# The order of a retention head's five projection blocks: v moved behind both gate blocks, and to second place in the last head

## The chip, the cores and the metric

The kernel runs on one core of a Trainium2 chip. The time is the device time of one execution in microseconds (us); smaller is better. Engines are named as the profile names them: PE (matmuls), PEld (the weight loads of PE), DVE, ACT, POOL, and SP, which here only issues DMAs. PSUM is the memory that matmuls write, SBUF the one that all engines read.

## The reference

A trunk of two layers on 1024 tokens of width 1024, in float32. What the change touches is the mixer of layer 1, a retention with 4 heads, of key width 256 and value width 512:

```python
def retention_mixer(xn, wq, wk, wv, wg, gn_gain, wo):
    ...
    q = (xn @ wq).reshape(Bn, S, RET_HEADS, RET_KDIM)
    k = (xn @ wk).reshape(Bn, S, RET_HEADS, RET_KDIM) * (RET_KDIM ** -0.5)
    v = (xn @ wv).reshape(Bn, S, RET_HEADS, RET_VDIM)
    o = chunkwise_retention(rotary(q, pos), rotary(k, pos), v)
    ...
    return (jax.nn.silu(xn @ wg) * o) @ wo
```

A head so has a `q` and a `k` of 256 columns, a `v` of 512 and a gate `g` of 512. The five projections of a head, and those of different heads, can be computed in any order.

## The kernel before, in words

**Blocks.** The projections of a head are five blocks of PE's work. `q`, `k`, and the gate in two halves (`g0` and `g2`, 256 columns each) are one call of `strassen` each: seven products of Strassen's scheme with 12 matmuls of 128x512 each, 84 in all. `values_block` computes `v`: seven products of 48 matmuls of 128x256. Every operand is split in a high and a low part: a cast on ACT (L109) and a subtraction on POOL or DVE (L110) make an `hl` tile out of a `raw` one (a weight as it was loaded) or an `s` tile (a sum or difference of weights, on DVE). PE starts on a product when its `hl` is there and its PSUM bank is free. The products of one block go into four banks (`b` or `o`, in turn by block), some banks twice; L284, L300, L305 and L311 are ACT's copies out of them into `u`, L289, L310, L312 and L315 are DVE's additions to `u`. L300 and L305 free banks that the same block uses again.

**Buffers.** `raw` has 5 slots (L126 loads one, SP issues), `hl` 7, `s` 3, `u` 5, and `h` one. `h` is used by the rotation and, as `extra`, by `values_block` for half of its sums.

**The rotation.** After `q` and after `k`, `rotated(h, s, us)` applies the rotary tables in two halves: DVE multiplies into `h` (L1151), adds into `u` (L1152, L1153), ACT casts and DVE subtracts (L109, L110, into `h`), and ACT issues the write of `h` to the scratch tensor `qscr` (L1158, 1 MB; for `k` two more writes of `u` to `kscr`, L1157, 256 KB each). Half 1 needs the same `h` tile, so it waits until half 0's `qscr` write has landed. PE is meanwhile in the next block. A gate block ends in two silu activations (L1324) and two writes to `scr` (L1325), and `v`'s results go to `vscr` (L1087, 512 KB each).

**Order.** All engines and queues take their instructions in order, and a scheduler has merged the blocks' steps: loads, casts and sums of the next block stand among the steps of the one that runs. Before, every head has the order `q`, `k`, `g0`, `v`, `g2`, with banks `b`, `o`, `b`, (`v` takes both), `o`. The very last `g2` is given to `last_block`, which frees parts of `xc` (the split activations) as it goes and fetches the first unit's `q`, `k`, `kf`, `v` from the scratch tensors (L1165, L1171, L1174, L1276).

**The units.** After the blocks the retention itself runs in eight units (4 heads, 2 halves of the tokens): `scores` (L1186 matmuls, L1191 on DVE, split into `sT`), `key_rows` (L1201 transposes, L1202 and L1203 into `ky`), `first_state` (L1212 matmuls, L1218 and L1219 into `st`), `outputs` (L1236 matmuls, L1240 statistics, L1227 scaling into `ky`), `gated` (L1260 transposes). Weights `wo` of the output projection are loaded beside them as `raw`.

Of the kernel before, what the change touches and what calls it, by code (L numbers as in the profile page):

```python
# [13 lines left out]
P = 128  # L14
# [60 lines left out]
def trunk(tc, a):  # L75
# [28 lines left out]
    def f(ap):  # L104
        return ap.bitcast(F32)

    def split(hi, lo, src, eng=None):

        act.copy(hi, src)  # L109
        (eng or pool).tensor_tensor(lo, src, f(hi), ALU.subtract)  # L110
# [227 lines left out]
    def run(gen):  # L338
        for _ in gen:
            pass  # L340
# [294 lines left out]
    def filler():  # L635
        for c in range(4):
            while at["heads"] <= c:
                yield
            yield from gated_conv(c)
        while at["values"] < 4 or at["pairs"] < 3:  # L640
            yield
        vp.close()
        xtp.close()
        mix["mp"] = Pool("mp")
        mix["ab"] = Pool("ab")
        gather((1, 3, 5, 7, 0, 2, 4), mix["ab"])
        for js in ((1, 3), (5, 7)):
            for _ in project(js, (1, 3, 5, 7, 0, 2, 4, 6), u_bank):
                yield from (None,) * 4

    steps = filler()
# [57 lines left out]
    def xc_tiles():  # L709
        return [xcp[b].tile([P, 2, 4, HALF], "xc", dt=F32R) for b in range(7)]  # L710
# [3 lines left out]
    def u_tile():  # L714
        return mp.tile([P, T], "u", 5)

    def h_tile():
        return mp.tile([P, 2, T], "h", dt=F32R)
# [65 lines left out]
    xc = xc_tiles()  # L784
# [251 lines left out]
    xc = nxt["xc"]  # L1036
# [105 lines left out]
    def rotated(h, s, us):  # L1142

        for half in range(2):
            tab = u_tile().rearrange("p (a t) -> p a t", a=2)
            sync.dma_start(out=tab, in_=a["c_rot"][h, half, :, 2 * s : 2 * s + 2, :])
            cs, sn = tab[:, 0, :], tab[:, 1, :]
            u0, u1 = (u[:, half * HALF : (half + 1) * HALF] for u in us)
            hl = h_tile().rearrange("p s (a t) -> p s a t", a=2)
            for i, (x, y) in enumerate(((u0, cs), (u1, sn), (u0, sn), (u1, cs))):  # L1150
                dve.tensor_tensor(f(hl[:, i // 2, i % 2]), x, y, ALU.mult)  # L1151
            dve.tensor_tensor(u0, f(hl[:, 0, 0]), f(hl[:, 0, 1]), ALU.subtract)  # L1152
            dve.tensor_tensor(u1, f(hl[:, 1, 0]), f(hl[:, 1, 1]), ALU.add)  # L1153
            for i, u in enumerate((u0, u1)):
                split(hl[:, 0, i], hl[:, 1, i], u, dve)
                if s == 1 and half == 0:
                    act.dma_start(out=kscr[h, :, i], in_=u)  # L1157
            act.dma_start(out=qscr[4 * h + 2 * half + s], in_=f(hl))  # L1158
# [106 lines left out]
    def wo_sweep(half, h, yT, g, tiles, after=None):  # L1265
        def lhs(j):
            return lambda s, t: yT[2 * g + j][:, s, (t - 4 * half) * P : (t - 4 * half + 1) * P]

        return sweep(
            [lhs(j) for j in range(2)], [w_rows(wo, h * 4 + 2 * g + j) for j in range(2)], tiles, o_bank, after  # L1270
        )
# [14 lines left out]
    def last_block(steps):  # L1286

        yield next(steps)
        close_xc(0)
        rt[0] = Pool("rt0")  # L1290
        unit0["q"] = fetch_q(0, 0)
        unit0["tri"] = wk.tile([P, HALF], "g", 2)
        sync.dma_start(out=unit0["tri"], in_=a["c_tri"])
        yield next(steps)
        close_xc(1)
        rt[1] = Pool("rt1")
        unit0["k"] = fetch_k(0, 0)
        yield next(steps)
        close_xc(6)
        rt[2] = Pool("rt2")  # L1300
        unit0["v"] = fetch_v(0, 0, sync)
        yield from steps
        close_xc(4, 3, 5, 2)
        rt[3] = Pool("rt3")
        rt[4] = Pool("rt4")

    blocks = [("ret_wq", 0), ("ret_wk", 0), ("ret_wg", 0), None, ("ret_wg", 2)]
    for h in range(4):
        for n, block in enumerate(blocks):
            if block is None:  # L1310
                run(values_block(h))
                continue
            name, i = block
            c0 = (h * (4 if name == "ret_wg" else 2) + i) * P
            us = []
            steps = strassen(a[name][0], c0, c0 + P, xc, Both, ((o_bank if n in (1, 4) else b_bank),), us, lay=1)
            if h == n == 0:
                steps, us = nxt["head"]
            run(last_block(steps) if (h, n) == (3, 4) else steps)
            if n < 2:  # L1320
                rotated(h, n, us)
                continue
            for j, u in enumerate(us):
                act.activation(u, u, AF.Silu)  # L1324
                act.dma_start(out=scr[4 * h + i + j], in_=u)  # L1325
# [5 lines left out]
    steps = iter(())  # L1331
    for n, (h, half) in enumerate(units):
# [24 lines left out]
        if more:  # L1357
            gt = fetch_g(*units[n + 1])
            tiles = range(4 * half, 4 * half + 4)
            steps = chain(*[wo_sweep(half, h, yT, g, tiles) for g in range(2)])  # L1360
# [3 lines left out]
    xc = xc_tiles()  # L1364
# [53 lines left out]
```

## Time and profile before

| | |
|---|---|
| time, median of 3 runs | 2725.92 us (2721.56 to 2728.98) |
| profiled execution | 2726.38 us, of which the span of the trace is 2724.6 us |
| PE busy | 2645.2 us, 97% of the span |
| DVE, ACT, POOL busy | 1915.8, 1189.9, 795.9 us |
| retention projections | 1243.8 to 1708.8 us of the span |

A row of the timeline has the start and the duration of an instruction, or of several alike in succession (x12), and in brackets the engine's idle time before it and what ended it. "<-ACT u L305" means that ACT's instruction of line 305, which wrote or read a `u` tile, came last.

### The profile page before, as it was taken

How to read it: one execution, taken by the hardware profiler on the slowest of the kernel's cores; microseconds unless marked ns; L12 is line 12 of the kernel's file. 1: busy time of each engine (PE TensorE's matmuls, PEld its weight loads, DVE VectorE, ACT ScalarE, POOL GpSimd, SP SyncE). 2: the span in 40 equal slices, each digit the busy share in tenths (PEclk: the TensorE clock that was granted, in tenths of full speed). 3: DMA queues.
4: the chain of work that ended last, by engine and by line, in shares of the span. 5: the costliest groups of instructions: out<-in, count | busy, mean ns of one | idle time of the engine just before them, and what ended most of it. 6: DMA issues, size and time to landing. Idle time of an engine off the chain costs nothing. (4 is left out here: it accounts for less than half of the span.)

```text
span 2724.6 us, 34990 instructions
## 1 busy us (share of the span) xinstructions
PE 2645.2 (97%) x12793; PEld 2166.0 (80%) x12793; DVE 1915.8 (70%) x2950; ACT 1189.9 (44%) x2050; POOL 795.9 (29%) x603
## 2 busy tenths in 40 slices
PE   8999999899999999989999999899999999999999
PEld 6877777778888888868888888788877888887887
DVE  4247776687777789697575765466678777777986
ACT  4345543454444444364444434222235444445444
POOL 6721113533333400032222122344454333331000
PEclk9999999999999999999999999899999999999999
DMA  5310012122222274424554546655422222225654
GB/s 171 104 48 28 24 35 79 38 75 89 74 89 74 86 266 154 152 84 160 176 178 151 195 150 219 244 210 186 155 73 60 78 85 72 88 74 187 206 174 154
DMA packets 258785, 336.74 MB, mean 124 GB/s; under 512 B 15121, under 2 KB 182197, under 8 KB 252469
## 3 DMA queue, kind: packets, MB, share of 16 engines
q1 hardware_dynamic: 224428, 246.94, 28.4%
q10 hardware_dynamic: 34184, 87.57, 8.8%
q8 instruction: 100, 1.64, 0.2%
q14 instruction: 73, 0.59, 0.1%
HBM read 257.38 MB, written 77.07 MB: 123 GB/s over the span
## 5 line engine op out<-in xcount | busy, mean ns | idle before, releaser
L110 POOL TENSOR_TENSOR hl<-raw,hl 128x512 fp32r<-128x512 f32 x347 | 580.9, 1688 | 1250.9 <-ACT hl L109 1231.0
L245 PE MATMUL b<-xc,hl 128*128 128x512 f32 (+1 forms) x2652 | 606.2, 388 | 10.7 <-ACT u L305 5.7
L245 PE MATMUL o<-xc,hl 128*128 128x512 f32 (+1 forms) x2568 | 590.7, 389 | 12.9 <-DVE hl L110 3.3
L245 PEld LDWEIGHTS b<-xc,hl 128*128 128x128 f32 x2652 | 485.9, 189 | 125.2 <-ACT u L305 7.0
L245 PEld LDWEIGHTS o<-xc,hl 128*128 128x128 f32 x2568 | 473.4, 190 | 123.6 <-DVE hl L110 4.2
L109 ACT CAST hl<-raw 128x512 fp32r<-128x512 f32 (+1 forms) x440 | 264.9, 609 | 508.7 <-PE o L328 151.7
L110 DVE TENSOR_TENSOR hl<-s,hl 128x512 fp32r<-128x512 f32 x309 | 223.6, 727 | 222.0 <-ACT hl L109 222.0
L972 DVE SCALAR_TENSOR_TENSOR u<-u,cc,u 128x1022 f32<-128x1022 f32 (+1 forms) x176 | 263.4, 1521 | 0.9
L109 ACT CAST hl<-s 128x512 fp32r<-128x512 f32 x309 | 189.7, 619 | 136.8 <-PE b L245 47.2
L458 PE MATMUL u<-xT,hl 128*128 128x512 f32 x576 | 166.1, 410 | 0.0
L328 PE MATMUL o<-hl,y 128*128 128x512 f32 x672 | 163.6, 397 | 0.0
L905 PE MATMUL o<-hl,hl 128*128 128x512 f32 x600 | 146.3, 394 | 5.0 <-DVE hl L110 3.5
L328 PEld LDWEIGHTS o<-hl,y 128*128 128x128 f32 x672 | 125.6, 188 | 29.4 <-POOL y L110 0.2
L905 PEld LDWEIGHTS o<-hl,hl 128*128 128x128 f32 x600 | 111.3, 188 | 34.4 <-DVE hl L110 7.1
L333 DVE TENSOR_TENSOR xb<-xb,o 128x512 f32<-128x512 f32 x160 | 105.0, 680 | 38.0 <-PE o L328 37.9
L458 PEld LDWEIGHTS u<-xT,hl 128*128 128x128 f32 x576 | 99.4, 189 | 20.7 <-issue 5.7
L970 ACT ACTIVATE u<-u,cc 128x1024 f32<-128x1024 f32 x88 | 100.9, 1151 | 31.3 <-DVE u L312 31.3
L109 ACT CAST hl<-h 128x512 fp32r<-128x512 f32 (+1 forms) x124 | 70.0, 581 | 95.0 <-PE o L905 28.2
L1063 PE MATMUL o<-hl,xc 128*128 128x256 f32 x768 | 95.4, 282 | 0.9 <-DVE hl L110 0.8
L1063 PEld LDWEIGHTS o<-hl,xc 128*128 128x128 f32 x768 | 93.8, 188 | 1.8 <-DVE hl L110 1.0
L110 DVE TENSOR_TENSOR hl<-h,hl 128x512 fp32r<-128x512 f32 (+1 forms) x124 | 78.4, 647 | 21.9 <-ACT hl L109 21.7
L152 POOL TENSOR_SCALAR rr<-ss 128x1 f32<-128x1 f32 (+1 forms) x48 | 13.8, 287 | 254.8 <-ACT s L163 235.9
(220 smaller groups left out, 4009.4 us busy)
## 6 DMA issues: line engine op xcount, KB each, us to landing
raw<-in_ffn_w_up SPq DMA_DIRECT2D x176, 256.0 KB, 3.1
raw<-in_ffn_w_down SPq DMA_DIRECT2D x176, 256.0 KB, 3.3
hs<-u ACTq DMA_DIRECT2D x44, 512.0 KB, 2.7
h<-hs SPq DMA_DIRECT2D x44, 512.0 KB, 6.4
raw<-in_even_w_in SPq DMA_DIRECT2D x73, 256.0 KB, 2.8
qscr<-h ACTq DMA_DIRECT2D x16, 1024.0 KB, 4.0
vscr<-u ACTq DMA_DIRECT2D x32, 512.0 KB, 3.8
raw<-in_ret_wo SPq DMA_DIRECT2D x64, 256.0 KB, 3.2
```

The source lines that it names most:

```text
L109: act.copy(hi, src)
L110: (eng or pool).tensor_tensor(lo, src, f(hi), ALU.subtract)
L152: pool.tensor_scalar(out, ss, 1.0 / n, EPS, ALU.mult, ALU.add)
L245: pe.matmul(u, hl[:, ws, k * P : (k + 1) * P], xc[b][:, xs, k, cols_], start=(first and k == 0 and i == 0), stop=(k == 3 and i == 2), skip ...
L328: pe.matmul(o, lhs[j](ls, t), ws[j][hf][:, w, :], start=(j == 0 and i == 0), stop=(j == n - 1 and i == 2),)
L333: dve.tensor_tensor(xs, xs, o, ALU.add)
L458: pe.matmul(u, hl(ws, k), xT[:, xs, k, hf * 512 : (hf + 1) * 512], start=(k == 0 and i == 0), stop=(k == KT - 1 and i == 2),)
L905: pe.matmul(o, l[:, ls, c * P : (c + 1) * P], r[:, ws, :], start=(start and i == 0), stop=(stop and i == 2), skip_group_check=True,)
L970: act.mul(c, u, wcol(2, jj))
L972: dve.scalar_tensor_tensor(c[:, d:], u[:, :-d], wcol(2 - d, jj), c[:, d:], ALU.mult, ALU.add)
L1063: pe.matmul(u[t // 2][:, c : c + 256], xc[b][:, xs, k, ts], hl[name][k // 2][:, ws, k % 2 * 256 : k % 2 * 256 + 256], start=(first and k = ...
```

## The change

Heads 0 to 2 now run `q`, `k`, `g0`, `g2`, `v`, with banks `b`, `o`, `b`, `o` and both. The last head runs `g0`, `v`, `q`, `k`, `g2`, with banks `b`, both, `o`, `b`, `o`. The rotation follows `q` and `k` wherever they stand, and `last_block` still gets the last head's `g2`. Lines behind the edit move by 3 (L1324 becomes L1327).

```diff
-    blocks = [("ret_wq", 0), ("ret_wk", 0), ("ret_wg", 0), None, ("ret_wg", 2)]
+
+    wq, wk_, wg0, wg2 = ("ret_wq", 0), ("ret_wk", 0), ("ret_wg", 0), ("ret_wg", 2)
+    blocks = [((wq, b_bank), (wk_, o_bank), (wg0, b_bank), (wg2, o_bank), (None, None))] * 3
+    blocks.append(((wg0, b_bank), (None, None), (wq, o_bank), (wk_, b_bank), (wg2, o_bank)))
     for h in range(4):
-        for n, block in enumerate(blocks):
+        for n, (block, kind) in enumerate(blocks[h]):
...
-            steps = strassen(a[name][0], c0, c0 + P, xc, Both, ((o_bank if n in (1, 4) else b_bank),), us, lay=1)
+            steps = strassen(a[name][0], c0, c0 + P, xc, Both, (kind,), us, lay=1)
...
-            if n < 2:
-                rotated(h, n, us)
+            if name != "ret_wg":
+                rotated(h, int(name == "ret_wk"), us)
                 continue
```

The instructions are the same in kind and, but for a few merged ones, in number; what changes is where they stand on each engine. First ACT in head 1's `g0` block, from the rotation's `qscr` write to the copy L305. Of before, `raw_12358` and `raw_12360` are slots with `v`'s weights; of the change, `raw_12337` is one with a weight of `g2` and `s_12340` a difference of its weights:

```order
 L1158 DMA qscr_10822<-h_12163 128x2048
 L300 COPY u_12211<-b_12213 128x512
-L109 CAST hl_12362<-raw_12358 128x512
-L109 CAST hl_12365<-raw_12360 128x512
+L109 CAST hl_12369<-raw_12337 128x512
+L109 CAST hl_12385<-s_12340 128x512
 L305 COPY u_12212<-b_12216 128x512
```

Two casts of `v`'s weights ahead of L305 have gone; casts for `g2` stand there.

Then DVE in head 0's `g2` block of the change, just behind the rotation of `k`. `raw_11269` and `s_11264` belong to `g2`, the other `raw` slots hold `v`'s weights, `h_11393` is the tile of `v`'s sums:

```order
L110 TENSOR_TENSOR hl_11342<-s_11265,hl_11342 128x512
L297 TENSOR_TENSOR s_11327<-raw_11269,s_11264 128x512
L1097 TENSOR_TENSOR s_11394<-raw_11402,raw_11404 128x512
L1098 TENSOR_TENSOR s_11395<-s_11394,raw_11397 128x512
L1099 TENSOR_TENSOR h_11393<-raw_11409,raw_11414 128x512
L1097 TENSOR_TENSOR h_11393<-raw_11414,raw_11416 128x512
L1098 TENSOR_TENSOR h_11393<-h_11393,raw_11409 128x512
L289 TENSOR_TENSOR u_11274<-u_11274,o_11277 128x512
L110 TENSOR_TENSOR hl_11358<-s_11327,hl_11358 128x512
```

and ACT in the same block:

```order
L305 COPY u_11275<-o_11279 128x512
L109 CAST hl_11358<-s_11327 128x512
L109 CAST hl_11399<-raw_11397 128x512
L109 CAST hl_11411<-raw_11409 128x512
L109 CAST hl_11425<-raw_11421 128x512
L109 CAST hl_11428<-raw_11423 128x512
L300 COPY u_11274<-o_11276 128x512
```

`raw_11414` takes the slot that L297 frees, `raw_11416` the one that L1097 of `s_11394` frees, `raw_11421` the one that L1097 of `h_11393` frees. Before, `v`'s loads and sums stood in the `g0` block and in `v` itself, and ahead of L300 in `g2` stood three casts of the next head's `q` weights.

Last, DVE from the end of the last `g2` block into the first unit; `u_14807`, `u_14808` and `h_14940` belong to the rotation of the last `k`, half 1:

```order
+L1153 TENSOR_TENSOR u_14808<-h_14940 128x512
 L310 TENSOR_TENSOR u_14973<-u_14973,o_14974 128x512
+L110 TENSOR_TENSOR h_14940<-u_14807,h_14940 128x512
 L315 TENSOR_TENSOR u_14972<-u_14972,o_14977 128x512
+L1191 TENSOR_TENSOR s_15137<-b_15130,g_15000 128x512
+L110 TENSOR_TENSOR h_14940<-u_14808,h_14940 128x512
 L312 TENSOR_TENSOR u_14973<-u_14973,o_14976 128x512
-L1191 TENSOR_TENSOR s_15137<-b_15130,g_15000 128x512
 L1191 TENSOR_TENSOR s_15148<-b_15141,g_15000 128x384
```

The rotation's last steps now stand among the first steps of the unit; before, that place had none of them. On ACT the four casts of `ky` (L1202) stand behind the four of `sT`, where before three of them stood ahead of the last.

## Rows read from the trace of the kernel before

**Rows 1.** The page's first part: the span, the busy time of the engines, and one of its costliest groups (PE's matmuls of the blocks with `b` banks: count, busy time, mean ns of one).

```profile
span 2724.6 us, 34990 instructions
...
PE 2645.2 (97%) x12793; PEld 2166.0 (80%) x12793; DVE 1915.8 (70%) x2950; ACT 1189.9 (44%) x2050; POOL 795.9 (29%) x603
...
L245 PE MATMUL b<-xc,hl 128*128 128x512 f32 (+1 forms) x2652 | 606.2, 388 | 10.7 <-ACT u L305 5.7
```

**Rows 2.** PE's waits from 1243.8 to 1708.8 us, the retention projections: total, how often, the longest.

```profile
PE b L245 <- ACT u L305: 5.7, 3, 2.6
PE b L245 <- ACT u L300: 1.4, 1, 1.4
PE o L1063 <- DVE hl L110: 0.8, 1, 0.8
PE o L1063 <- ACT hl L109: 0.2, 1, 0.2
```

**Rows 3.** The engines' busy time by stretches, here head 3's blocks: length, busy time (instructions) of each engine, granted clock, DMA share, GB/s.

```profile
1567.20:1708.80 141.60, 138.95 (x759) 119.38 (x758) 84.06 (x119) 57.53 (x98) 31.32 (x23) 1.00 0.56 193
```

**Rows 4.** PE's timeline, the rows of the blocks `g0` of heads 0 to 3 behind their waits, and the first matmuls of head 1's `v`.

```profile
1278.91 4.48 PE L245 MATMUL b<-xc,hl 128*128 128x512 f32 x18 [1.43 <-ACT u L300]
...
1403.49 3.07 PE L245 MATMUL b<-xc,hl 128*128 128x512 f32 x12 [1.73 <-ACT u L305]
1406.40 0.87 PE L1063 MATMUL o<-hl,xc 128*128 128x256 f32 x6
...
1524.08 3.06 PE L245 MATMUL b<-xc,hl 128*128 128x512 f32 x12 [1.31 <-ACT u L305]
...
1646.00 3.07 PE L245 MATMUL b<-xc,hl 128*128 128x512 f32 x12 [2.65 <-ACT u L305]
```

**Rows 5.** ACT's timeline in the `g0` blocks of heads 0, 1 and 3.

```profile
1278.27 0.59 ACT L300 COPY u<-b 128x512 f32<-128x512 f32 x1 [2.16 <-DVE h L110]
...
1401.71 1.24 ACT L109 CAST hl<-raw 128x512 fp32r<-128x512 f32 x2 [4.54 <-DMA raw<-in_ret_wv]
1402.86 0.58 ACT L305 COPY u<-b 128x512 f32<-128x512 f32 x1
...
1408.33 0.33 ACTq L1158 DMA_DIRECT2D qscr<-h  x1
...
1644.22 1.24 ACT L109 CAST hl<-raw 128x512 fp32r<-128x512 f32 x2 [4.43 <-DMA raw<-in_ret_wv]
```

**Rows 6.** DVE's timeline in head 0 (`g0`, then `v`) and in head 1's `g0`.

```profile
1283.80 3.58 DVE L1151 TENSOR_TENSOR h<-u,u 128x512 f32<-128x512 f32 x4 [5.94 <-issue]
...
1291.52 0.68 DVE L110 TENSOR_TENSOR hl<-s,hl 128x512 fp32r<-128x512 f32 x1
...
1296.04 0.69 DVE L1097 TENSOR_TENSOR h<-raw,raw 128x512 f32<-128x512 f32 x1 [3.12 <-DMA qscr<-h]
...
1396.71 0.68 DVE L1099 TENSOR_TENSOR s<-raw,raw 128x512 f32<-128x512 f32 x1
```

**Rows 7.** The DMAs issued from 1243.8 to 1708.8 us: count, size of each, median us from issue to landing.

```profile
qscr<-h ACTq DMA_DIRECT2D x16, 1024.0 KB, 4.0
vscr<-u ACTq DMA_DIRECT2D x32, 512.0 KB, 3.8
raw<-in_ret_wv SPq DMA_DIRECT2D x47, 256.0 KB, 3.9
...
raw<-in_ret_wg SPq DMA_DIRECT2D x28, 256.0 KB, 3.2
...
kscr<-u ACTq DMA_DIRECT2D x8, 256.0 KB, 2.5
```

**Rows 8.** DVE's timeline in the first unit.

```profile
1710.44 0.69 DVE L1191 TENSOR_TENSOR s<-b,g 128x512 f32<-128x512 f32 x1
...
1726.63 1.29 DVE L1219 TENSOR_TENSOR st<-o,st 128x512 fp32r<-128x512 f32 x2 [10.31 <-ACT st L1218]
```

**Rows 9.** PE's timeline in the first unit.

```profile
1708.88 3.92 PE L1186 MATMUL b<-q,k 128*128 128x512 f32 x24
...
1713.87 0.74 PE L1212 MATMUL o<-v,ky 128*128 128x512 f32 x2 [0.39 <-ACT ky L1202]
...
1730.55 0.47 PE L1260 MATMUL b<-ident,ky 128*128 128x128 f32 x1 [3.29 <-DVE ky L1227]
1732.40 0.48 PE L1260 MATMUL b<-ident,ky 128*128 128x128 f32 x1 [1.38 <-DVE ky L1227]
1734.99 1.75 PE L1260 MATMUL b<-ident,ky 128*128 128x128 f32 x7 [2.11 <-DVE ky L1227]
1737.57 1.75 PE L1260 MATMUL b<-ident,ky 128*128 128x128 f32 x7 [0.83 <-DVE ky L1227]
```

**Rows 10.** SP's timeline in the first unit.

```profile
1715.51 0.83 SPq L126 DMA_DIRECT2D raw<-in_ret_wo  x2
```

**Rows 11.** ACT's timeline in the first unit.

```profile
1725.49 0.62 ACT L109 CAST hl<-raw 128x512 fp32r<-128x512 f32 x1 [7.67 <-DMA raw<-in_ret_wo]
```

**Rows 12.** The engines' busy time by stretches of 4 us around the first unit; columns as in the third group.

```profile
1728.00:1732.00 4.00, 0.47 (x1) 0.18 (x1) 2.65 (x6) 0.00 (x0) 1.48 (x4) 0.75 1.05 413
1732.00:1736.00 4.00, 1.49 (x6) 1.20 (x7) 2.73 (x6) 0.00 (x0) 0.90 (x3) 0.50 0.25 97
```

## The prediction

> **What bounds the kernel now.** I first read the busy time of the engines: PE works 2645.2 of 2724.6 us [rows 1], so only PE's idle time can be won or lost by an order. Then PE's waits, for the retention projections alone (1243.8 to 1708.8 us): 5.7 us for `u` at L305 in three waits, 1.4 us for `u` at L300 in one, and 0.8 + 0.2 us for `hl` in a `v` block [rows 2]: 8.06 us with the second decimals of the timeline, 0.30% of the time. That is all that an order of these blocks can win while the work stays the same (the granted clock is 1.00 in the stage [rows 3]). The timeline of PE says where they are: each of the four `g0` blocks stops once, 1.43, 1.73, 1.31 and 2.65 us in heads 0 to 3 [rows 4]; the `k` blocks, the `g2` blocks and the start of the next head's `q` do not stop.
>
> Why `g0` stops is in ACT's timeline. L305, the copy that lets PE reuse a PSUM bank, stands behind casts of the next block's weights, and with `v` next these wait for a load that is late: head 1's casts wait 4.54 us for `raw`, run at 1401.71, and L305 follows at 1402.86 (head 3: 4.43 us) [rows 5]. The load is late because its slot is one of five and was freed only by the DVE step at 1396.71, behind the rotation of `k` [rows 6]. 1396.71 + 0.68 to 1401.71 is 4.3 us, and the stage's loads of `in_ret_wv` take 3.9 us from issue to landing in the median [rows 7]. In head 0 it is L300 that waits, for DVE's rotation step (2.16 us [rows 5]).
>
> **Heads 1 and 2: `g0` loses its wait, `g2` gets one.** Ahead of L305 now stand a cast of a `g2` weight, loaded long before, and of an `s` tile; so 1.73 and 1.31 us go. The eight early loads of `v` move into the `g2` block. There, L300 stands behind the cast of a `raw` slot that the `h` step of L1097 frees, and that step waits for an earlier slot, freed by L1097 of `s`: two loads in series. Head 1: DVE's rotation tail ends near 1408 [rows 5]; four more steps, 0.6 us apart, end with L1097 of `s` at 1410.3. A load takes 3.6 us (between the stage's medians for `in_ret_wg`, 3.2, and `in_ret_wv`, 3.9 [rows 7]): it lands at 1413.9, its use ends at 1414.5, the second lands at 1418.1, a cast and L300 of 0.6 us each end at 1419.3. PE starts this block at 1403.49 + 3.07 - 1.73 = 1404.8 and needs L300 after 60 of its 84 matmuls, at 606.2 / 2652 = 0.229 us each [rows 1] 13.7 us later: 1418.5. New wait 0.8 us (0 to 4). Net -0.9 for head 1. Head 2 has the same steps in the same order; I take a wait of 1.0 us, net -0.3.
>
> **Head 0: a longer chain.** Its DVE does the rotation later (half 1 starts 5.94 us after the step before it), and at 1291.52 is at the first `hl` step behind the rotation [rows 6]. From there DVE goes hl, hl, L297, L1097: 1293.9. One load, 3.6 us, and L1097 of `h` at 1298.1; second load at 1301.7; two casts and L300: 1303.5; 1 us less since POOL no longer casts beside the rotation. PE, whose `g0` ends at 1278.91 + 4.48 = 1283.4 [rows 4], arrives after 64 matmuls, at 1298.0. 1302.5 - 1298.0: it waits 4.5 us, in one piece or two (its `s4` product first waits for an `hl` step behind the same L1097). Bounds 3.7 and 6.1, by loads of 3.2 and 4.4 us. What goes is 0.94 us in `v` (DVE then waited 3.12 us for `qscr` [rows 6]); the 1.43 us stay, as ACT's order up to L300 is unchanged. Net +3.6.
>
> **Head 3.** Its `g0` runs first, with no rotation before it, so the slots for `v`'s loads come free without it: 2.65 us go. In `v`, `q` and `k` behind it I find no new wait: no chain of loads stands behind a rotation there but the one into the last `g2`, whose four loads need no second round.
>
> **The first unit.** `k`'s rotation now lies in the last `g2` block, and its tail runs into the unit that follows. In head 1 that tail ended (issue of `qscr`, ACT) at 1408.33, 1.9 us after the block's end at 1406.40 [rows 4, 5]; without the block's own wait of 1.73 it is 3.7 us. On DVE two `h` steps stand among the first L1191, on ACT the casts of `ky` come behind all of `sT`. L1191 was done first at 1710.44 [rows 8], 1.6 us after the block's end, so the unit's matmuls start 3.7 - 1.6 = 2.1 to 5 us later. What hides this: PE has 3.29 + 1.38 + 2.11 + 0.83 = 7.6 us idle later in this unit [rows 9], waiting for a chain that starts with the cast at 1725.49, when the `wo` load issued at 1715.51 [rows 10] has landed [rows 8, 11]. So the slip itself costs nothing; the landing of `wo` decides. And here is a new load: `k`'s rotation writes 2 x 1 MB of `qscr` and 0.5 MB of `kscr` in that block, where before 1 MB of `vscr` was left. The engines that move the data were full up to 1732, at 413 GB/s [rows 12]; 1.5 MB are 3.6 us. Some of that falls before the `wo` load is issued and some transfers of later units now go behind it. Bounds 0 and +6 (3.6 and the part of the slip that is not hidden); I take +2. The clock is at 0.50 (1.2 GHz) from 1732 [rows 12] and may fall a little earlier or later; that lies inside the bounds.
>
> On that load the Trainium skill ("DMA: Bandwidth & Descriptors", section "Issuing engines are not separate DMA queues") says that transfers issued by different engines run on the same 16 engines and interleave. It speaks against this change, as ACT's writes then delay SP's `wo`; the trace agrees so far as both queues together fill the share to 1.0 there. By the rule the full 1.5 MB would count, and the sum would come 1.6 us higher; were the queues independent, 2 us lower.
>
> **Sum.** Head 0 +3.6, head 1 -0.9, head 2 -0.3, head 3 -2.65, first unit +2: +1.75 us on the profiled execution's 2726.38, which is 0.02% over the median of the runs: 2728 us. PE's work, DMAs, casts and subtractions are the same in number; the few moved silu activations on ACT and `scr` writes have an engine that is idle for most of the stage [rows 3] in front of them.
>
> **Rivals.** (a) The waits go and nothing replaces them: the loads in `g2` are in time. For it: SP has free slots sooner if the rotation ends sooner. Against: five slots, and two loads in series behind DVE. It gives 2726.4 - 8.06 + 1.43 (head 0's stays) = 2719.7. (b) Slower: loads into `g2` collide with the rotation's `qscr` and `scr` writes in the same microseconds and take 5.5 us instead of 3.6. For it: `qscr` writes themselves take 4.0 in the median [rows 7], and head 0's half 1 waited 5.94 us for one [rows 6]. Three heads x two loads x 1.9 = +11.4: 2739.5. It decides from loads of 4.6 us on (six times 1.0 us are the distance to 0.3%). (c) The first unit slips in full, its start 5 us and `wo` 3.6 us, not overlapped: 2728.1 - 2 + 8.6 = 2734.7. (d) The moves cancel everywhere, as the same loads and steps are only permuted: 2726.
>
> **How the numbers follow.** A measurement of this kernel tells about 0.3% (8.2 us) from no change: the bounds are 2717.7 and 2734.1. Forecast (2723 to 2733) 0.58; (a) 0.12, of which half passes the bound when head 0's wait goes too; (b) 0.17; (c) 0.08; (d) 0.05. Faster 0.06; slower (b) with most of (c) less their smaller sizes, 0.19; the same 0.75. The range leaves out the far half of (a) and of (b): 2719 to 2738.
>
> **What would show it.** Right: no wait for L305 in the `g0` of heads 1 to 3; about 4.5 us of PE waits in head 0's `g2`, about 1 us for L300 in those of heads 1 and 2; the first L1212 of the first unit 2 to 5 us later after the block's end and the `wo` cast some 2 us later. Wrong: no waits in `g2` (then (a)); loads of `in_ret_wv` of over 4.6 us there (then (b)); a `wo` cast that is later by over 4 us (then (c)); PE waits in the blocks of head 3, for which I have no term.

## The result, and the profile after

| | before | after |
|---|---|---|
| median of 6 runs each, us | 2725.98 (2721.56 to 2728.98) | 2733.90 (2733.57 to 2736.45) |
| profiled execution: time / span, us | 2726.38 / 2724.6 | 2733.86 / 2731.8 |
| first `o` matmul of head 0's `q`, us from the span's start | 1243.79 | 1246.11 |
| first matmul of head 1 | 1345.38 | 1353.32 |
| head 1 / 2 / 3, us | 121.00 / 120.58 / 121.92 | 120.31 / 119.94 / 119.02 |
| first scores (L1186) of the first unit | 1708.88 | 1712.59 |
| from there to the second unit's scores, us | 30.09 | 34.63 |
| from there to the span's end, us | 985.63 | 984.58 |

The ratio is 1.0035 (interval 1.0025 to 1.0045): the change made the kernel slower by about 0.35%, where 2728 us had been forecast. The marks in the table are the starts of matmuls in PE's timeline; the difference of 7.2 us in span is +7.94 up to the end of head 0, -0.69, -0.64 and -2.90 in heads 1 to 3, +4.54 in the first unit and -1.05 behind it. So the heads behind the first did what was forecast, and two places cost about twice what they were given. One run further on, of the last head alone, took 3086.88 us at a granted clock of 0.787 and is left out of that experiment's median and ratio.

The page's first part after; PE's work grows by 2.7 us only, so most of the loss is idle time.

```profile
span 2731.8 us, 35003 instructions
...
PE 2647.9 (97%) x12793; PEld 2165.8 (79%) x12793; DVE 1906.5 (70%) x2950; ACT 1189.9 (44%) x2050; POOL 795.7 (29%) x603
```

PE's waits after, from 1200 to 1760 us (total, how often, the longest), those of the stage and of the first unit.

```profile
PE b L1201 <- DVE s L1191: 7.5, 3, 4.6
PE o L245 <- ACT u L300: 4.7, 4, 1.9
PE o L245 <- DVE hl L110: 4.1, 2, 4.0
...
PE b L1260 <- DVE ky L1227: 3.0, 2, 1.6
...
PE o L1212 <- ACT ky L1202: 1.2, 1, 1.2
```

The 5.7 us for L305 of [rows 2] are gone. In their place stand waits on an `o` bank, which is the bank of `g2`, and in the first unit the wait for L1191, of which the kernel before had 0.2 us.

**Head 0's `g2`.** PE's timeline after: the last pieces of `g2` in head 0, then in heads 1 and 2.

```profile
1303.17 0.73 PE L245 MATMUL o<-xc,hl 128*128 128x512 f32 x2 [3.96 <-DVE hl L110]
1305.77 7.41 PE L245 MATMUL o<-xc,hl 128*128 128x512 f32 x20 [1.87 <-ACT u L300]
...
1427.60 5.88 PE L245 MATMUL o<-xc,hl 128*128 128x512 f32 x24 [1.03 <-ACT u L300]
...
1547.55 5.88 PE L245 MATMUL o<-xc,hl 128*128 128x512 f32 x24 [0.68 <-ACT u L300]
```

DVE's timeline after, the steps ahead of that `hl`, and below it ACT's.

```profile
1297.93 1.58 DVE L1099 TENSOR_TENSOR h<-raw,raw 128x512 f32<-128x512 f32 x1 [3.39 <-DMA raw<-in_ret_wv]
1299.44 1.75 DVE L1097 TENSOR_TENSOR h<-raw,raw 128x512 f32<-128x512 f32 x1
...
1302.43 0.69 DVE L110 TENSOR_TENSOR hl<-s,hl 128x512 fp32r<-128x512 f32 x1
```

```profile
1304.02 1.21 ACT L109 CAST hl<-raw 128x512 fp32r<-128x512 f32 x2 [5.91 <-DMA raw<-in_ret_wv]
1305.14 0.58 ACT L300 COPY u<-o 128x512 f32<-128x512 f32 x1
```

SP's timeline, the loads from the first of the two rounds on.

```profile
1293.24 12.97 SPq L126 DMA_DIRECT2D raw<-in_ret_wv  x7
```

This is the forecast chain: a load, DVE's `h` steps, a second load into the slot they free, the cast, L300. SP issues the first load at 1293.24 and the second at 1301.21, each within 0.03 us of the end of the DVE step that frees its slot (L297, and L1097 into `h`). From its issue to the step that waits for it the first takes 4.7 us and the second 2.8; in heads 1 and 2 the pairs are 5.6 and 2.8, and 4.9 and 2.9. PE waits 3.96 + 1.87 = 5.83 us in it. Heads 1 and 2 have the short form of it (1.03 and 0.68). What the forecast lacked is in the second row of PE: 20 matmuls take 7.41 us, where 24 take 5.88 in head 1, which is 4.9 for 20. The windows after say why (columns as in [rows 3]: length, busy time of PE, PEld, DVE, ACT and POOL, granted clock, DMA share, GB/s).

```profile
1304.00:1308.00 4.00, 2.23 (x5) 1.83 (x6) 1.70 (x2) 2.21 (x4) 2.51 (x2) 0.55 0.60 184
1308.00:1312.00 4.00, 4.00 (x12) 3.13 (x11) 1.20 (x3) 0.62 (x1) 0.00 (x0) 0.59 0.69 216
1312.00:1316.00 4.00, 4.00 (x31) 3.77 (x30) 3.21 (x5) 3.12 (x4) 0.00 (x0) 1.00 0.08 32
```

Behind the two waits the granted clock is 0.55 and 0.59, mostly the lower of its two levels (1.2 GHz), and 1.00 again from 1312 on. PE is busy all through the second window, so no list of waits shows these 2.5 us.

**The first unit.** DVE's timeline after, the two halves' last and first steps in the rotation of head 3's `k` and the first L1191.

```profile
1702.11 1.78 DVE L110 TENSOR_TENSOR h<-u,h 128x512 fp32r<-128x512 f32 x1
1714.94 2.50 DVE L1151 TENSOR_TENSOR h<-u,u 128x512 f32<-128x512 f32 x4 [11.06 <-issue]
...
1720.36 0.68 DVE L1191 TENSOR_TENSOR s<-b,g 128x512 f32<-128x512 f32 x1
```

ACT's timeline after, in the same place.

```profile
1703.92 0.33 ACTq L1158 DMA_DIRECT2D qscr<-h  x1
...
1718.14 0.33 ACTq L1276 DMA_DIRECT2D v<-vscr  x1
...
1729.58 1.14 ACT L109 CAST hl<-raw 128x512 fp32r<-128x512 f32 x2 [1.06 <-DMA qscr<-h]
...
1734.42 1.27 ACT L1218 CAST st<-o 128x512 fp32r<-128x512 f32 x2 [3.71 <-PE o L1212]
```

And PE's.

```profile
1712.59 3.93 PE L1186 MATMUL b<-q,k 128*128 128x512 f32 x24
1721.10 0.69 PE L1201 MATMUL b<-ident,kf 128*128 128x128 f32 x2 [4.58 <-DVE s L1191]
1722.77 1.11 PE L1201 MATMUL b<-ident,kf 128*128 128x128 f32 x4 [0.97 <-DVE s L1191]
1725.82 0.69 PE L1201 MATMUL b<-ident,kf 128*128 128x128 f32 x2 [1.94 <-DVE s L1191]
1727.75 7.32 PE L1212 MATMUL o<-v,ky 128*128 128x512 f32 x24 [1.25 <-ACT ky L1202]
...
1747.22 4.05 PE L1186 MATMUL b<-q,k 128*128 128x512 f32 x24 [0.19 <-DVE gt L1261]
```

The two halves use one and the same `h` tile. Half 0's last step ends at 1703.89, ACT issues the 1 MB write of that tile at 1703.92, and half 1's first product starts at 1714.94, 11.0 us later: DVE stands for the write to land (the profile calls it "issue", since no instruction releases it). The trace's semaphore records have that write landing at 1714.87, and in the run with seven slots the profile names it, in DVE's timeline:

```profile
1707.37 2.50 DVE L1151 TENSOR_TENSOR h<-u,u 128x512 f32<-128x512 f32 x4 [10.07 <-DMA qscr<-h]
```

In the median of the stage such a write lands in 4.0 us [rows 7], the slowest of the sixteen in 8.2 by the same records; here the engines that move the data were full. L1191 queues behind half 1 on DVE, so L1212 starts 15.2 us behind the scores; before it was 5.0 [rows 9]. The `wo` load, which ended the waits there before [rows 11], is cast at 1729.58, and ACT then waits 3.71 us for PE's L1212: it no longer decides.

Three of the windows after: full transfer engines while the write is in flight and behind it, and PE's clock at its lower level once PE has waited.

```profile
1706.00:1710.00 4.00, 4.00 (x18) 3.20 (x17) 0.00 (x0) 1.10 (x2) 3.38 (x3) 1.00 1.03 416
...
1714.00:1718.00 4.00, 2.52 (x19) 2.38 (x17) 3.06 (x6) 0.00 (x0) 0.00 (x0) 1.00 1.06 422
...
1722.00:1726.00 4.00, 1.30 (x5) 0.86 (x6) 1.33 (x4) 1.57 (x2) 1.26 (x1) 0.50 1.04 423
```

On the shared engines the Trainium skill ("DMA: Bandwidth & Descriptors", section "Issuing engines are not separate DMA queues") says that transfers issued by different engines interleave on the same 16 engines; the trace agrees, with ACT's write at 11.0 us among SP's fetches, where 4.0 was the median in the stage before.

### The profile page after: what moved, and what is told of

The parts are those of the page before. It is cut to its first block, busy times and chain, and to the rows that moved or that the text cites. A ratio compares the mean times of both kernels' runs of the same rounds, so it can differ in the third digit from the quotient of the medians.

```text
span 2731.8 us, 35003 instructions
## 1 busy us (share of the span) xinstructions
PE 2647.9 (97%) x12793; PEld 2165.8 (79%) x12793; DVE 1906.5 (70%) x2950; ACT 1189.9 (44%) x2050; POOL 795.7 (29%) x603
```

## The experiments

The theory is that the loss has two places that have nothing to do with each other: head 0's `g2`, whose loads go one behind the other through five slots, and the first unit, where half 1 of the last rotation waits for half 0's write. The rivals: only one of the two costs anything and the other is covered by idle time behind it, as the forecast had it for the unit's start; or the first unit is late by the landing of `wo`, as the forecast also had it. Times stand against runs of the kernel before on the same chip, with medians of 2724.5 to 2725.4 us.

**Heads 0 to 2 alone.** The last head keeps the old order.

```diff
-    blocks.append(((wg0, b_bank), (None, None), (wq, o_bank), (wk_, b_bank), (wg2, o_bank)))
+    blocks.append(((wq, b_bank), (wk_, o_bank), (wg0, b_bank), (None, None), (wg2, o_bank)))
```

> Heads 0 to 2 in the changed order, the last head in the old one. If the loss has two sources (head 0's wait in g2 with the clock that falls behind it, and the first unit), this keeps the first alone: new waits of 5.8 + 1.0 + 0.7 us and about 2.6 us of slow matmuls in head 0, less 1.4 + 0.9 + 1.7 + 1.3 us of old ones: +4.8, about 2731. The rival, that the loss lies wholly at the end of the stage: 2724 to 2726. The first unit as in the kernel before: 30.1 us from its first scores to the second unit's.

Measured 2731.72 us, ratio 1.0023 (1.0013 to 1.0033). Head 1 starts at 1352.56. PE's timeline of this run has the same two waits in head 0's `g2`:

```profile
1303.38 1.22 PE L245 MATMUL o<-xc,hl 128*128 128x512 f32 x2 [3.94 <-DVE hl L110]
1306.03 6.38 PE L245 MATMUL o<-xc,hl 128*128 128x512 f32 x20 [1.42 <-ACT u L300]
```

The first unit takes 30.0 us, as before. So head 0's loss is whole without the last head, and nothing later hides it.

**The last head alone.** Heads 0 to 2 in the old order.

```diff
-    blocks = [((wq, b_bank), (wk_, o_bank), (wg0, b_bank), (wg2, o_bank), (None, None))] * 3
+    blocks = [((wq, b_bank), (wk_, o_bank), (wg0, b_bank), (None, None), (wg2, o_bank))] * 3
```

> Heads 0 to 2 in the old order, the last head in the changed one. By two sources: head 3 loses its 2.65 us, the first unit gains 4.5 us: about 2728, with half 1 of the last rotation waiting some 11 us on DVE. The rival, that the first unit costs nothing by itself but only because the three heads before it shift the transfers: 2723.5, and the rotation's half 1 waits for about 4 us.

Measured 2727.79 us, ratio 1.0008 (0.9999 to 1.0017). Head 1 starts at 1345.05, the scores come 3.4 us sooner (1705.51), and the unit takes 34.21 us. DVE's timeline of this run, with the write issued at 1697.03:

```profile
1707.40 2.50 DVE L1151 TENSOR_TENSOR h<-u,u 128x512 f32<-128x512 f32 x4 [10.40 <-issue]
```

So the +4 of the unit belongs to the last head's order and comes without head 0's delay; what the head's own blocks gain pays for most of it.

**Another order, `v` first.** Head 0 in the old order, the others `v`, `q`, `k`, `g0`, `g2`: no rotation stands next to `v`'s loads, and none runs into the first unit.

```diff
-    blocks = [((wq, b_bank), (wk_, o_bank), (wg0, b_bank), (wg2, o_bank), (None, None))] * 3
-    blocks.append(((wg0, b_bank), (None, None), (wq, o_bank), (wk_, b_bank), (wg2, o_bank)))
+    blocks = [((wq, b_bank), (wk_, o_bank), (wg0, b_bank), (None, None), (wg2, o_bank))]
+    blocks += [((None, None), (wq, b_bank), (wk_, o_bank), (wg0, b_bank), (wg2, o_bank))] * 3
```

> Head 0 in the old order, heads 1 to 3 in the order v, q, k, g0, g2: v always stands behind two gate blocks, the last g2 has no rotation in it, head 0 is untouched. By two sources neither loss appears: the waits of heads 1 to 3 for L305 go (5.7 us), g2 of heads 1 and 2 wait 0.7 to 1.0 us each: about -4, 2722. The rival, that any order with v behind g2 pays for its loads as much as it gains: 2726.

Measured 2723.62 us, ratio 0.9996 (0.9988 to 1.0005). The scores come at 1704.57, 4.3 us sooner than before, but the unit takes 32.13 us and PE waits 5.29 us at L1260: `wo` is cast 18.7 us behind the scores (16.6 before). Without half 1's wait the landing of `wo` sets the unit, and gives back part of what the stage won.

**Half 1 in its own tile.** After, with half 1 of the last rotation in the second `q` tile of `rt0`, so that it doesn't wait for half 0's write; `last_block` runs it once that pool is open.

```diff
-            hl = h_tile().rearrange("p s (a t) -> p s a t", a=2)
+            hl = tile if tile is not None else h_tile().rearrange("p s (a t) -> p s a t", a=2)
...
         unit0["q"] = fetch_q(0, 0)
+        rotated(3, 1, unit0["us"], (1,), rt[0].tile([P, 2, 2, HALF], "q", 2, dt=F32R))
```

> The changed kernel, with half 1 of the last rotation in a tile of its own (the one that unit 1's q is fetched into later), so that it needn't wait for half 0's write. If that wait makes the first unit late: DVE starts half 1 right behind half 0, the first unit takes about 30 us instead of 34.6, and the time is about 2729.5. If the added bytes on full transfer engines make it late, as the prediction had it: no change or slower, 2733 to 2735, as the same bytes move and unit 1's q is fetched later.

Measured 2735.29 us, ratio 1.0034 (1.0021 to 1.0046). From DVE's, SP's and ACT's timelines of this run:

```profile
1702.83 2.48 DVE L1151 TENSOR_TENSOR q<-u,u 128x512 f32<-128x512 f32 x4
```

```profile
1709.09 0.37 SPq L1281 DMA_DIRECT2D gt<-scr  x1
1718.05 0.32 SPq L1165 DMA_DIRECT2D q<-qscr  x1
```

```profile
1734.61 1.27 ACT L109 CAST hl<-raw 128x512 fp32r<-128x512 f32 x2 [12.56 <-DMA raw<-in_ret_wo]
```

The wait is gone and L1212 starts 5.0 us behind the scores, as before. Yet the unit takes 36.44 us: the second unit's `q` fetch finds its tile taken, holds SP's queue until 1718.05, and the `wo` loads stand behind it. Taking the named wait away wins nothing here, since the landing of `wo` is next; how much of that is the queue, this run alone can't say.

**Half 0's write from other tiles.** After, with half 0's `qscr` written from the `u` tiles, so that `h` is free for half 1; the low parts of half 0 of this one `k` are left out of the computation.

```diff
+            if (h, s, half) == (3, 1, 0):
+                for p in range(2):
+                    for i, u in enumerate((u0, u1)):
+                        act.dma_start(out=qscr[4 * h + 2 * half + s, :, p, i], in_=u)
+                continue
```

> The changed kernel, but the write of half 0 of the last head's k takes the same 1 MB from the u tiles (four writes of 256 KB) instead of from h, so that h is free for half 1 at once; bytes and SP's order stay. What is left out: that half's low parts in the scratch tensor are copies of its unsplit values. If half 1's wait for the write delays the first unit: no wait of over 1 us at the last L1151, the first L1212 some 5 us after the first scores instead of 15, and the unit 30 to 31.5 us instead of 34.6: about 2730. If the bytes on the full transfer engines delay it as well, through the wo load: the start is early, but the wo cast comes 18 us or more after the first scores and the unit stays at 33 to 36 us: 2733 or more.

Measured 2736.09 us, ratio 1.0040 (1.0028 to 1.0053). Half 1 starts at 1701.69 without a wait. ACT's timeline shows where the time is now:

```profile
1718.25 9.27 ACTq L1333 DMA_DIRECT2D scr<-u  x2
1727.56 1.34 ACT L109 CAST sT<-s 128x512 fp32r<-128x512 f32 x3 [8.32 <-DMA gt<-scr]
```

Each of the two issues of the `scr` writes takes 0.33 us, at 1718.25 and 1727.19; the row's 9.27 us run from the first to the end of the second. Between them ACT stands, with the casts of `sT` and `ky` behind it, and the profile names SP's fetch of `gt` as what ended that. SP's timeline:

```profile
1707.16 0.37 SPq L1286 DMA_DIRECT2D gt<-scr  x1
```

That fetch reads other rows of `scr` than the write fills, and the first write did not wait for it. In the trace's records the second write has the same semaphore as the fetch, which lands at 1727.12 by it; the issue follows 0.07 us later. So one queue here stands for another's transfer, 20 us in flight on full engines. As a repair this fails, and it doesn't price the half's wait.

**A later `v`, in three orders.** Every unit's `v` goes into one tile, so that the 2 MB of the second unit's `v` are fetched only when the first unit is done with its own. The edit is the same in all:

```diff
-        v = rt[4 if half else 2].tile([P, 2, 4, HALF], "v", dt=F32R)
+        v = rt[2].tile([P, 2, 4, HALF], "v", dt=F32R)
```

With `v` first:

> The order with v first in heads 1 to 3, and every unit's v fetched into the one tile, so that unit 1's 2 MB are no longer fetched while the first unit waits for wo. If the landing of wo sets the first unit: it lands some 4 us sooner, the unit takes 28 to 29 us instead of 32.1, and the time is about 2720. If the unit is set by DVE's statistics behind st: no change, 2723.6. Against it: later units may wait for their v.

With the order before:

> The kernel before, with every unit's v fetched into the one tile as in the run beside it. If the landing of wo sets the first unit here too: the cast that stood at 16.6 us behind the first scores comes at 12 to 13, the unit takes 27 us instead of 30.1, about 2722. If not: 2724.6.

With the order after:

> The kernel after, with the second half's v of each unit put in the same tile as the first half's, so that 2 MB of unit 1's v are loaded later. Theory (the first unit costs +4.5 because the last k's half 1 waits for half 0's 1 MB write on transfer engines that are full, and the wo landing stands behind that): if the 2 MB of v are not among the transfers of that window the write lands in less than the 11.0 us, but unit 0's own transfers and the write are still there, so half 1 is still late; the unit from first scores to the next unit's scores shrinks from 34.6 to 29 to 32 us, and the time comes to 2727 to 2730. Head 0 stays at its +7. Rival (the wo landing has nothing to do with this unit any more, only the half's wait, and that write is slow because of unit 0's own loads): the unit stays at 34 us and the time at 2731 to 2734, less what later units gain.

| order | time, us | ratio | unit, us (without the edit) | `wo` cast behind the scores, us (without) |
|---|---|---|---|---|
| `v` first | 2716.28 | 0.9966 (0.9954 to 0.9978) | 27.35 (32.13) | 13.9 (18.7) |
| before | 2717.48 | 0.9970 (0.9959 to 0.9982) | 24.79 (30.09) | 11.8 (16.6) |
| after | 2732.75 | 1.0031 (1.0019 to 1.0042) | 33.90 (34.63) | not waited for |

In the first two orders the landing of `wo` behind 2 MB of `v` sets the unit: 5 us each. In the order after it does not, and the same edit is worth 0.7 us of the unit. DVE's timeline of that run:

```profile
1713.75 2.50 DVE L1151 TENSOR_TENSOR h<-u,u 128x512 f32<-128x512 f32 x4 [10.70 <-issue]
```

I had expected the write to land sooner with less `v` in flight. It takes 10.7 us all the same, but this is no test of what makes it slow: in the order after, the second unit's `v` was issued only at 1718.14, when the write had landed. What is in flight with the write are the first unit's own fetches: after, SP issues `q`, `k`, `kf` and two parts of `v` from 1695.92 to 1701.9, 4.5 MB, with `gt` from 1707.14. By the trace's semaphore records `kf` lands at 1706.4, the parts of `v` at 1710.8 and 1714.3, and the write at 1714.9; at the 344 to 422 GB/s of the windows some 4.4 MB, an estimate, moved while it was in flight, 1 MB of them its own. That these fetches hold the write up is worked out, not tried.

**Both limits of the unit in one run.** Half 1 in its own tile, the late `v`, and the second unit's `q` in the tile that the late `v` leaves empty.

```diff
-        q = rt[0].tile([P, 2, 2, HALF], "q", 2, dt=F32R)
+        q = rt[4 if (h, half) == (0, 1) else 0].tile([P, 2, 2, HALF], "q", 1 if (h, half) == (0, 1) else 2, dt=F32R)
```

> The kernel after with three edits of the first unit at once: half 1 of the last k's rotation writes into the second q tile (no wait for half 0's write), unit 1's q goes into a tile of the pool that the late v leaves empty (so SP's queue does not stop at it), and each unit's v is in one tile. Theory (the first unit costs +4.5 by two limits in series, half 1's wait, and behind it the landing of wo; each alone leaves the other in place): with both gone the unit from first scores to the next unit's scores is 24 to 28 us instead of 34.6 (25 in the order before with the late v alone), and the time 2724 to 2728. Head 0 keeps its +7. Rival (a third limit holds this order's unit, its own writes on full transfer engines, so that the write of half 1 keeps every later fetch back): 31 us or more, 2730 or more.

Measured 2728.47 us, ratio 1.0012 (1.0003 to 1.0021). The unit takes 30.42 us, between what the two theories gave. L1212 starts 4.6 us behind the scores. ACT's timeline:

```profile
1729.14 0.62 ACT L109 CAST hl<-raw 128x512 fp32r<-128x512 f32 x1 [11.01 <-DMA raw<-in_ret_wo]
```

So the unit is 4.2 us shorter than that of the change, and 3.5 us shorter than with the late `v` alone: that much at least came of half 1's wait. But `wo` is cast 17.0 us behind the scores, as late as before the change, although 2 MB of `v` are out of its way and SP issues it 4.4 us behind the scores (6.6 before). From its issue at 1716.51 to the cast it takes 12.6 us, where the order before with the late `v` has 7.4. Which transfers hold it there I have not taken apart; the new one is the 1 MB write of half 1, issued at 1709.82. So the second limit was still there.

**Seven slots for the raw weights.** After, with two more; the rest of the program's plan shifts too.

```diff
-RAW = 5
-HL = 7
+RAW = 7
+HL = 6
```

> The changed kernel with 7 raw slots instead of 5 and 6 hl instead of 7 (there is no room for more); the scheduler moves steps all over the program, so that only the g2 blocks of heads 0 to 2 are read. If head 0's waits there come from two loads in series through five slots: PE's waits of 5.8 us in head 0's g2 fall to under 3 us, those of heads 1 and 2 (1.0 and 0.7) to nothing. If they come from DVE's late rotation alone: head 0 keeps over 5 us.

Measured 2725.65 us, in a single run. In head 0's `g2` no wait is left, head 1 starts at 1345.66 (1345.38 before the change), and in heads 1 and 2 PE waits 0.34 us. So with slots enough the order costs nothing in head 0, as loads that follow each other through five slots would have it; since the plan shifts too, this isn't an edit of one thing alone. The unit still takes 38.55 us, with L1201 waiting 5.78: more slots don't touch that.

**The best of these together.** `v` first, late `v`, seven slots.

> The order v, q, k, g, g from head 1 on with the late v (2716.3 so far), with seven slots for raw weights instead of five and six for hl instead of seven. Theory (waits in the stage come from loads that go in series through five slots): this order has only 1.7 us of such waits left in heads 1 to 3 and head 0's, so seven slots can take at most 3 to 4 us: 2712.5 to 2716. Rival (the slots shift the plan of the stages ahead as well, or six hl slots bring waits of their own): 2717 or more.

Measured 2708.28 us, ratio 0.9942 (0.9930 to 0.9955), faster than both kernels. PE's waits of this run from 1243 to 1760 us are these two and no others:

```profile
PE b L1260 <- DVE ky L1227: 3.0, 2, 1.6
PE b L245 <- ACT u L300: 0.6, 1, 0.6
```

By the medians that is 8.0 us better than with five slots (7.6 when each is set against the kernel before on its own chip), and 6.3 us in span, where I had put 3 to 4 at most. In the stage little was won, as the waits there were small: 459.0 us from entry to scores with five slots, 457.5 with seven. The unit takes 23.1 us instead of 27.35, and what lies behind it is 2.4 us shorter. That the slots would help the unit I had not expected, and I have not taken it apart.

## Why the prediction was nearly right and too low

The range held the time; the likeliest case, 2728, missed it by 6 us, and the chance of "no change" was too high. Step by step:

- **What bounds the kernel, heads 1 to 3**: right, in the sizes of `g2` partly by luck (see the rivals). The L305 waits go, and new ones of 1.03 and 0.68 us come in `g2` (forecast 0.8 and 1.0). Forecast -0.9, -0.3, -2.65; measured -0.69, -0.64, -2.90.
- **Head 0, "a longer chain" (+3.6)**: the mechanism was right; the trace has its chain step by step, and the seven-slot run, in which more than the slots changes, speaks for the same cause. The size was off. The wait is 5.83 us, inside the given bounds of 3.7 to 6.1, but by another sum. The second load began at 1301.2, where 1298.1 was forecast: 0.4 us of that by the first load, 2.7 by DVE's `h` steps, two of 1.58 and 1.75 us where the forecast had one of 0.6. It then came 0.8 us sooner than the forecast 3.6 us, and the 1 us that POOL was to give back did not show: L300 ended at 1305.7, not 1302.5. PE in turn arrived at 1299.2, not 1298.0, as the forecast took the end of `g0` from a row that ends with its window, at 18 matmuls; all 24 take 5.88 us, and the block behind them starts at 1284.6, not at 1283.4. Not in the sum at all: the 2.5 us of PE at the lower clock behind the wait (by the same count 1.3 to 2.8 us in the six runs with this order and five slots). The 0.94 us in `v` do go: 5.83 + 2.5 - 0.94 = 7.4 from the end of `g0` on, where the marks give 7.1. The other 0.8 us of the 7.94 lie ahead of it: the stage's entry came 2.3 us later, and the 1.43 us in `g0`, which the forecast had kept, were not there (in the run with its own tile, entered at 1243.57, they are 1.33). Across the runs with five slots head 1 starts at 1344.1 to 1346.1 in the five where head 0 has the old order, and at 1351.4 to 1353.3 in the six with the new one: 5.3 us apart at the least, 9.2 at the most.
- **The first unit (+2)**: this is the step that failed. "So the slip itself costs nothing; the landing of `wo` decides": the slip is not 2.1 to 5 us but 10, and is itself the limit: L1218 now waits 3.71 us for L1212, where before it stood behind the cast of `wo`. The forecast took the rotation's tail from head 1, where such a write has the stage's median of 4.0 us, and the 413 GB/s of the unit's own windows [rows 12] only for `wo`; it did not ask which step of the tail waits for a transfer. Half 1 does, for 11.0 us. The late `v` in the order after shows that `wo` no longer decides (0.7 us), and the last head alone that the loss is there without head 0's. That the value, +4.5, lay inside the bounds 0 to +6 is luck.
- **The rivals**: (c), 2734.7, came nearest by time, with a late start of the unit as it said, but not with a late `wo`. (b) came in half: in heads 0 to 2 the first of the two loads, issued 0.7 us behind the start of the two `scr` writes, took 4.7, 5.6 and 4.9 us, over its 4.6, and the second 2.8, 2.8 and 2.9. The two together are 7.5, 8.4 and 7.8 us against the 7.2 of the forecast and the 11 of (b), so two errors in the forecast cancel. (a) fell, except in the kernel with seven slots.
- **The rule on shared engines** (the Trainium skill, "DMA: Bandwidth & Descriptors"): by it the unit was to be 1.6 us dearer. The sign was right, and the first thing that it made late was the write itself, not `wo`.

Open: why in the run against both limits `wo` is cast 17 us behind the scores, and how the stage's entry differs between executions of the same code.

## What to carry to other kernels

When a step is moved, go through its instructions for one that waits for a transfer, a tile reused behind its own write above all, and price that transfer at the load of the place where it goes, not of the place it comes from: here 4.0 us became 11. When a wait of several microseconds is added to PE, add the time in which the matmuls behind it run at the lower clock (here 2.5 us behind 5.83). And idle time further on covers a slip only if it ends with something that doesn't start later as well; taking one limit away is worth what the next one leaves, as the own tile (no gain) and the late `v` (7 us in two orders, 1 in the third) show.

## What the runs showed that I had not expected

- From the issue of half 0's 1 MB write in the last block to half 1's start it was 11.0, 10.4, 10.7 and 11.2 us (the change, the last head alone, the change with the late `v`, the seven slots), where the stage's median to landing is 4.0.
- The same code up to that point enters the stage between 1243.44 and 1246.68 us in different executions, with no order of the five blocks to tell them apart.
- An issue on ACT can stand for a transfer of SP with which it shares no data: in the run with half 0's write from other tiles a `scr` write of 0.33 us came 8.9 us behind the one before it, when SP's fetch of `gt` on the same semaphore had landed.
